# Column pieces of 704, 192 and 128 for the last row, and sums of their own in place of running sums

## The chip, the cores and the metric

The kernel runs on one core of one Trainium2 chip. The metric is the time of one execution in microseconds (us) on the device. Before the change it was 164.64 us (median of 3 runs, 164.58 to 164.67). A second measure is the **tail**, the time from the landing of row 14 of the last tile to the moment the store is issued. Both ends are in every trace, the landing as the last increment of that load's semaphore.

## The reference

```python
def reference(x):                      # x: (32, 512, 1024) float32
    relu_x = np.maximum(x, 0)
    return np.mean(relu_x, axis=-1).astype(np.float32)      # (32, 512)
```

16,384 rows of 1,024 numbers: each of the 128 partitions (the first dimension of every on-chip tile) takes 128 rows.

## The kernel before

Seven tiles of 16 rows stream in whole, and an eighth, the last one, in pieces. Rows alternate between ScalarE (`act_row`) and VectorE (`dve_row`); each is one instruction that applies the relu and adds up the row. Both engines follow it with a short instruction that reads the accumulator out. The last tile's pieces are of 8, 4, 2 and 1 rows, and its last row comes in column pieces, so that little work is left when the last byte has landed.

```python
def dve_row(nc, src, acc, init=None):
    nc.vector.tensor_scalar(out=src, in0=src, scalar1=0.0, scalar2=init,
                            op0=ALU.max, op1=ALU.add, accum_out=acc)
# ... (cut: tiles, loads of whole tiles)
    row_pieces = [8, 4, 2, 1]
    col_pieces = [512, 256, 256]
# ... (cut: the loads are issued here; rows 0 to 13 of the last tile)
    act_row(nc, prev[:, :512], part[:, 0:1])               # row 14, half each
    dve_row(nc, prev[:, 512:], part[:, 1:2])
    nc.gpsimd.tensor_scalar(out=res[:, J - 2:J - 1], in0=part[:, 0:1], scalar1=part[:, 1:2], scalar2=inv, op0=ALU.add, op1=ALU.mult)
    act_row(nc, last[:, :256], part[:, 2:3])               # row 15, piece 1
    dve_row(nc, last[:, 256:512], part[:, 3:4])
    nc.gpsimd.tensor_scalar(out=part[:, 4:5], in0=part[:, 2:3], scalar1=inv, scalar2=0.0, op0=ALU.mult, op1=ALU.add)
    act_row(nc, last[:, 512:640], part[:, 5:6])            # piece 2
    dve_row(nc, last[:, 640:768], part[:, 6:7], init=part[:, 3:4])
    nc.scalar.activation(out=part[:, 7:8], in_=part[:, 5:6], func=ACT.Identity, scale=inv, bias=part[:, 4:5])
    dve_row(nc, last[:, 768:], part[:, 8:9], init=part[:, 6:7])   # piece 3
    nc.vector.scalar_tensor_tensor(out=res[:, J - 1:J], in0=part[:, 8:9], scalar=inv, in1=part[:, 7:8], op0=ALU.mult, op1=ALU.add)
    nc.sync.dma_start(out=outr, in_=res)
```

The sums of VectorE form a chain: piece 2 starts from the sum of piece 1 (`init`), piece 3 from that of piece 2.

## Time and profile before

| what | value | where read |
|---|---|---|
| span of the profiled execution | 162.6 us | head of the page |
| DMA | 84% of the chain that ended last, 413 GB/s | chain, slices |
| VectorE, ScalarE busy | 46%, 43% | busy table |
| landing of row 14 | 157.81 us | semaphore records |
| landings of the three column pieces, after row 14's | +0.641, +0.994, +1.300 us | semaphore records |
| store issued, after row 14's landing (the tail) | +2.340 us | timeline |

From the page of the kernel before, the DMA engines' busy share in 40 slices of the span, in tenths, with what they moved, and below it the chain that ended last, first by engine and then by line:

```profile
DMA  7979989989988997997997998997998997998980
...
DMA packets 2162, 67.19 MB, mean 413 GB/s; under 512 B 240, under 2 KB 624, under 8 KB 880
```

```profile
DMA 84%; DVE 13%; SPq 1%; issue 0%; DVEq 0%
DMA xt<-in_x_dram 84%; DVE xt L20 13%; SPq L80 1%; SPq L72 0%; DVE res L112 0%; DVEq L20 0%; DVEq L112 0%
```

In the chain, a q behind an engine's name means its sequencer (SPq is that of SyncE), and L20 is the line inside `dve_row`. The DMA row stands at 0.7 or more in all but the last slice: the load stream sets the time. The change doesn't touch the stream, only its last 512 KB and what is computed on them. So everything at stake lies in the tail, 2.3 us of 162.6. Its timeline before (start in us, duration, engine, line, operation, out<-in; in brackets the idle time before, with its releaser):

```profile
157.83 0.69 DVE L20 TENSOR_SCALAR_CACHE_REDUCE xt<-xt 128x512 f32<-128x512 f32 x1
...
158.44 0.08 DVE L20 DVE_READ_ACCUMULATOR xt<-xt 128x1 f32 x1
...
158.47 0.42 DVE L20 TENSOR_SCALAR_CACHE_REDUCE xt<-xt 128x256 f32<-128x256 f32 x1
...
158.82 0.08 DVE L20 DVE_READ_ACCUMULATOR xt<-xt 128x1 f32 x1
...
158.93 0.35 DVE L20 TENSOR_SCALAR_CACHE_REDUCE xt<-xt,part 128x128 f32<-128x128 f32 x1
159.06 0.19 POOL L103 TENSOR_SCALAR part<-part 128x1 f32<-128x1 f32 x1
...
159.21 0.08 DVE L20 DVE_READ_ACCUMULATOR xt<-xt,part 128x1 f32 x1
159.32 0.48 DVE L20 TENSOR_SCALAR_CACHE_REDUCE xt<-xt,part 128x256 f32<-128x256 f32 x1
159.36 0.29 ACT L108 ACTIVATE part<-part 128x1 f32<-128x1 f32 x1
159.73 0.08 DVE L20 DVE_READ_ACCUMULATOR xt<-xt,part 128x1 f32 x1
159.92 0.16 DVE L112 SCALAR_TENSOR_TENSOR res<-part 128x1 f32<-128x1 f32 x1
160.15 0.35 SPq L115 DMA_DIRECT2D out_dram<-res  x1
```

Read it by VectorE (DVE). The second number of a reduction is longer than the time it holds the engine: the accumulator read starts before the reduction's record ends. What counts is from start to the start of the read: 613 ns for 512 columns, 345 for 256. A reduction that takes a running sum (`xt,part`) starts only after the read before it has ended, and takes 404 ns where the independent one of the same size took 345. Piece 3 landed at 159.11 us, but VectorE came to it at 159.32. Once it has begun on the last row, right on the first piece's landing (158.45), VectorE never again waits for data. GpSimd (L103) and ScalarE (L108) end by 159.66, with slack.

### The profile page before, as it was taken

How to read it: one execution, taken by the hardware profiler on the slowest of the kernel's cores; microseconds unless marked ns; L12 is line 12 of the kernel's file. 1: busy time of each engine (PE TensorE's matmuls, PEld its weight loads, DVE VectorE, ACT ScalarE, POOL GpSimd, SP SyncE). 2: the span in 40 equal slices, each digit the busy share in tenths (PEclk: the TensorE clock that was granted, in tenths of full speed). 3: DMA queues.
4: the chain of work that ended last, by engine and by line, in shares of the span. 5: the costliest groups of instructions: out<-in, count | busy, mean ns of one | idle time of the engine just before them, and what ended most of it. 6: DMA issues, size and time to landing. Idle time of an engine off the chain costs nothing.

```text
span 162.6 us, 358 instructions
## 1 busy us (share of the span) xinstructions
DVE 74.8 (46%) x135; ACT 69.6 (43%) x134; POOL 1.2 (1%) x8
## 2 busy tenths in 40 slices
DVE  0000039900696008940099201990049800698993
ACT  3000039700694008920099002980049600696882
POOL 0000000000000000000000000000000000000001
DMA  7979989989988997997997998997998997998980
GB/s 258 516 322 451 516 355 419 516 371 403 516 387 387 516 435 339 516 435 339 516 484 326 484 484 355 451 500 339 451 500 355 435 516 306 451 435 379 415 334 17
DMA packets 2162, 67.19 MB, mean 413 GB/s; under 512 B 240, under 2 KB 624, under 8 KB 880
## 3 DMA queue, kind: packets, MB, share of 16 engines
q1 hardware_dynamic: 2160, 67.18, 96.2%
q14 instruction: 2, 0.02, 0.0%
HBM read 67.11 MB, written 0.07 MB: 413 GB/s over the span
## 4 chain that ended last, share of the span: by engine, by line
DMA 84%; DVE 13%; SPq 1%; issue 0%; DVEq 0%
DMA xt<-in_x_dram 84%; DVE xt L20 13%; SPq L80 1%; SPq L72 0%; DVE res L112 0%; DVEq L20 0%; DVEq L112 0%
## 5 line engine op out<-in xcount | busy, mean ns | idle before, releaser
L20 DVE TENSOR_SCALAR_CACHE_REDUCE xt<-xt 128x1024 f32<-128x1024 f32 (+1 forms) x65 | 73.7, 1195 | 85.1 <-DMA xt<-in_x_dram 84.8
L15 ACT ACTIVATE xt<-xt 128x1024 f32<-128x1024 f32 (+1 forms) x66 | 67.0, 1016 | 89.2 <-DMA xt<-in_x_dram 89.2
L15 ACT ACTIVATION_READ_ACCUMULATOR xt<-xt 128x1 f32 x66 | 12.3, 187 | 0.0
L20 DVE DVE_READ_ACCUMULATOR xt<-xt 128x1 f32 x65 | 5.4, 83 | 0.0
L65 POOL TENSOR_SCALAR res<-sums 128x112 f32<-128x112 f32 (+1 forms) x2 | 0.5, 252 | 157.2 <-DVE xt L20 157.2
L15 ACT ACT_TABLE_LOAD x1 | 1.3, 1283 | 0.7 <-PEq L130 0.7
L20 DVE TENSOR_SCALAR_CACHE_REDUCE xt<-xt,part 128x128 f32<-128x128 f32 (+1 forms) x2 | 0.8, 412 | 0.1
L108 ACT ACTIVATE part<-part 128x1 f32<-128x1 f32 x1 | 0.3, 294 | 0.1
L98 POOL TENSOR_SCALAR res<-part 128x1 f32<-128x1 f32 x1 | 0.3, 264 | 0.6 <-ACT xt L15 0.6
L112 DVE SCALAR_TENSOR_TENSOR res<-part 128x1 f32<-128x1 f32 x1 | 0.2, 159 | 0.1
L103 POOL TENSOR_SCALAR part<-part 128x1 f32<-128x1 f32 x1 | 0.2, 191 | 0.1
L20 DVE DVE_READ_ACCUMULATOR xt<-xt,part 128x1 f32 x2 | 0.2, 83 | 0.0
L130 POOL MEMSET const-bfloat16-1.0<- 128x1 bf16 x1 | 0.1, 101 | 0.0
L130 POOL MEMSET const-uint8-127<- 128x1 uint8 x1 | 0.1, 101 | 0.0
L130 POOL MEMSET const-float32-0.0<- 128x1 f32 x1 | 0.1, 98 | 0.2 <-issue 0.2
L130 POOL MEMSET const-float32-1.0<- 128x1 f32 x1 | 0.1, 98 | 0.0
## 6 DMA issues: line engine op xcount, KB each, us to landing
xt<-in_x_dram SPq DMA_DIRECT2D x1, 4096.0 KB, 39.0
xt<-in_x_dram SPq DMA_DIRECT2D x1, 2048.0 KB, 43.5
xt<-in_x_dram SPq DMA_DIRECT2D x1, 1024.0 KB, 45.5
xt<-in_x_dram SPq DMA_DIRECT2D x1, 512.0 KB, 46.4
xt<-in_x_dram SPq DMA_DIRECT2D x1, 256.0 KB, 46.5
xt<-in_x_dram SPq DMA_DIRECT2D x2, 128.0 KB, 42.7
xt<-in_x_dram SPq DMA_DIRECT2D x7, 49.0
out_dram<-res SPq DMA_DIRECT2D x1, 64.0 KB, 1.5
```

Source lines behind the costliest of these rows:

```text
L15: nc.scalar.activation(out=src, in_=src, func=ACT.Relu, accum_out=acc)
L20: nc.vector.tensor_scalar(out=src, in0=src, scalar1=0.0, scalar2=init, op0=ALU.max, op1=ALU.add, accum_out=acc,)
L65: nc.gpsimd.tensor_scalar(out=res[:, lo:hi], in0=sums[:, lo:hi], scalar1=inv, scalar2=0.0, op0=ALU.mult, op1=ALU.add,)
L80: nc.sync.dma_start(out=xt[:, lo:lo + n, :], in_=xr[:, j0 + lo:j0 + lo + n, :])
L98: nc.gpsimd.tensor_scalar(out=res[:, J - 2:J - 1], in0=part[:, 0:1], scalar1=part[:, 1:2], scalar2=inv, op0=ALU.add, op1=ALU.mult,)
L103: nc.gpsimd.tensor_scalar(out=part[:, 4:5], in0=part[:, 2:3], scalar1=inv, scalar2=0.0, op0=ALU.mult, op1=ALU.add,)
L108: nc.scalar.activation(out=part[:, 7:8], in_=part[:, 5:6], func=ACT.Identity, scale=inv, bias=part[:, 4:5],)
L112: nc.vector.scalar_tensor_tensor(out=res[:, J - 1:J], in0=part[:, 8:9], scalar=inv, in1=part[:, 7:8], op0=ALU.mult, op1=ALU.add,)
L130: nc = _bacc.Bacc("TRN2", target_bir_lowering=False, num_devices=1)
```

## The change

Its intent: a smaller last piece (128 columns), no running sums on VectorE, no ScalarE work behind the first piece, and GpSimd adding up the parts beside VectorE's last reduction.

```diff
-    col_pieces = [512, 256, 256]
+    col_pieces = [704, 192, 128]
@@
-    act_row(nc, last[:, :256], part[:, 2:3])
-    dve_row(nc, last[:, 256:512], part[:, 3:4])
+    act_row(nc, last[:, :416], part[:, 2:3])
+    dve_row(nc, last[:, 416:704], part[:, 3:4])
+    dve_row(nc, last[:, 704:896], part[:, 4:5])
     nc.gpsimd.tensor_scalar(
-        out=part[:, 4:5], in0=part[:, 2:3], scalar1=inv, scalar2=0.0, op0=ALU.mult, op1=ALU.add,
+        out=part[:, 5:6], in0=part[:, 4:5], scalar1=part[:, 3:4], scalar2=part[:, 2:3], op0=ALU.add, op1=ALU.add,
     )
-    act_row(nc, last[:, 512:640], part[:, 5:6])
-    dve_row(nc, last[:, 640:768], part[:, 6:7], init=part[:, 3:4])
-    nc.scalar.activation(
-        out=part[:, 7:8], in_=part[:, 5:6], func=ACT.Identity, scale=inv, bias=part[:, 4:5],
-    )
-    dve_row(nc, last[:, 768:], part[:, 8:9], init=part[:, 6:7])
-    nc.vector.scalar_tensor_tensor(
-        out=res[:, J - 1:J], in0=part[:, 8:9], scalar=inv, in1=part[:, 7:8], op0=ALU.mult, op1=ALU.add,
+    dve_row(nc, last[:, 896:], part[:, 6:7])
+    nc.vector.tensor_scalar(
+        out=res[:, J - 1:J], in0=part[:, 6:7], scalar1=part[:, 5:6], scalar2=inv, op0=ALU.add, op1=ALU.mult,
     )
```

## The prediction

> What bounds it now. The page's chain that ended last is 84% load, 13% VectorE; the slice table shows the DMA engines at 0.8 to 1.0 and 413 GB/s to the end, while VectorE is busy 46% and ScalarE 43%. Only the tail can move, from row 14's landing (157.81 us by the trace's semaphore records) to the store's issue at 160.15, 2.3 us of a 162.6 us span.
>
> The tail before, from the timeline and the semaphore records. The column pieces landed at 158.45, 158.80 and 159.11. VectorE ran 512 columns of row 14 (157.83), 256 (158.47, right on its landing), 128 with a running sum (158.93), 256 with a running sum (159.32), the closing operation (159.92 to 160.08); the store issued at 160.15. After the last landing VectorE needed 0.98 us. ScalarE's and GpSimd's parts were done by 159.66, with slack.
>
> What the change does.
> 1. Landings. Rows of 2048, 1024 and 512 B took 84, 46 and 27 ns each in the trace; 2816 B and 768 B should take about 112 and 36 (estimate by interpolation), eight rows per engine. The same total; the landings become about 158.67, 158.93, 159.12. The first piece comes 0.22 us later, the last unchanged.
> 2. VectorE. A reduction with no running sum reaches its accumulator read after 80 ns plus n columns/0.96 ns (613 ns at 512, 345 at 256), and the next independent one starts there. A running-sum operand costs 59 ns more (404 against 345 at 256) and about 110 ns waiting for the earlier read; both go away. So (estimates) 288 columns 158.69 to 159.07, 192 to 159.34, 128 to 159.56, read done 159.64. Before, the last read was done at 159.81. The Trainium skill's "VectorE: DVE Perf Modes" (The TRN2 errata) states a fixed latency per SBUF instruction plus columns at 0.96 GHz; the trace agrees in slope, with 80 ns for its 58 cycles. VectorE gets 608 columns of the last row instead of 640, in three instructions either way.
> 3. ScalarE. 416 columns end with their read at 159.32, off the path.
> 4. GpSimd. The add waits for the 192-column sum, read at 159.42. Earlier GpSimd operations with two waits started 0.15 us after their last input, and took 0.19 us without and 0.26 with one per-partition operand; with two I estimate 0.33. So 159.57 to 159.91, and the closing operation starts about 159.97, not at 159.75 where VectorE alone would allow it. This is the new critical step, and takes back 0.2 us. The skill's "Perfetto Trace Analysis" (GPSIMD Engine Instruction) calls such spans unreliable, so this is my least sure term.
> 5. Closing operation: a per-partition operand, about 0.16 + 0.06 = 0.22 us, ending near 160.19, 0.1 us later than now. The store has one wait fewer ahead of it (0.03 us saved), issue near 160.22.
>
> Net: +0.07 us: VectorE's gain (0.17) is lost to GpSimd's late add. Predicted 164.7 us; 8 in 10 between 164.3 and 165.1 (mostly run and chip variation). Faster by over 2%: 0.01; within 2%: 0.98; slower by over 2%: 0.01.
>
> Shown right or wrong by: three VectorE reductions of the last row back to back with no gap; the closing operation released by GpSimd; VectorE idle about 0.2 us between its last accumulator read and the closing operation; first landing near 158.67, last near 159.12; store issue within 0.15 us of 160.2.
>
> What would make it wrong: GpSimd starting or finishing 0.2 us faster, which would make it about 0.1 us faster than before; landings of odd-sized rows (2816, 768 B) costing more than interpolated; the loads, 157 us, differing between runs by more than the whole tail.

## The result

The changed kernel took 164.69 us (median of 4 runs, 164.59 to 165.03); the kernel before, in the same rounds, 164.65 (4 runs). The ratio is 1.0007, with a 95% interval of 0.9989 to 1.0024: the same within what these runs resolve. (A ratio is the mean time of one kernel's fast runs over that of the other's of the same rounds, so it is not quite the ratio of the medians.) Five further rounds (e1) gave 1.0010 (0.9998 to 1.0022).

The load stream is unchanged: 413 GB/s over the span, before and after. The traces resolve more than the times. The tail grew from 2.340 to 2.476 us. From the page after, the chain by engine and line:

```profile
DMA 84%; DVE 12%; SPq 1%; issue 0%; POOLq 0%; DVEq 0%
DMA xt<-in_x_dram 84%; DVE xt L20 12%; SPq L80 1%; POOLq L137 0%; SPq L72 0%; DVE res L108 0%; DVEq L20 0%; POOLq L104 0%
```

GpSimd's sequencer (POOLq L104, the wait ahead of its add, and POOLq L137, a line of the launch code, which runs beside the add) has entered the chain, which it was not part of before; the end of the kernel now passes through it. The list of waits after names who waited for whom (us in total, times, longest):

```profile
POOL part L104 <- DVE xt L20: 0.7, 1, 0.7
...
DVE res L108 <- POOL part L104: 0.4, 1, 0.4
```

The tail after, to be held against the timeline before:

```profile
158.82 0.45 DVE L20 TENSOR_SCALAR_CACHE_REDUCE xt<-xt 128x288 f32<-128x288 f32 x1 [0.21 <-DMA xt<-in_x_dram]
159.20 0.08 DVE L20 DVE_READ_ACCUMULATOR xt<-xt 128x1 f32 x1
159.20 0.35 DVE L20 TENSOR_SCALAR_CACHE_REDUCE xt<-xt 128x192 f32<-128x192 f32 x1
...
159.47 0.08 DVE L20 DVE_READ_ACCUMULATOR xt<-xt 128x1 f32 x1
159.47 0.28 DVE L20 TENSOR_SCALAR_CACHE_REDUCE xt<-xt 128x128 f32<-128x128 f32 x1
159.68 0.08 DVE L20 DVE_READ_ACCUMULATOR xt<-xt 128x1 f32 x1
159.73 0.36 POOL L104 TENSOR_SCALAR part<-part 128x1 f32<-128x1 f32 x1 [0.68 <-DVE xt L20]
160.13 0.21 DVE L108 TENSOR_SCALAR res<-part 128x1 f32<-128x1 f32 x1 [0.37 <-POOL part L104]
160.37 0.35 SPq L111 DMA_DIRECT2D out_dram<-res  x1
```

VectorE now does 288, 192 and 128 columns with no gap: each reduction starts at the instant the accumulator read before it starts. But it first sits idle 0.21 us for the first piece, and after its last sum it sits idle 0.37 us before the closing operation, which waits for GpSimd's add (0.36 us long); that could start only when the 192-column sum had been read out.

Measured from each trace's own landing of row 14, in us:

| step | before | after, predicted | after, measured |
|---|---|---|---|
| first column piece landed | 0.641 | 0.86 | 0.900 |
| last column piece landed | 1.300 | 1.31 | 1.301 |
| VectorE's last accumulator read ended | 2.005 | 1.83 | 1.863 |
| GpSimd's add started, ended | | 1.76, 2.10 | 1.836, 2.201 |
| closing operation started, ended | 2.117, 2.276 | 2.16, 2.38 | 2.235, 2.448 |
| store issued (tail) | 2.340 | 2.41 | 2.476 |

The row of the predicted column is the prediction's time less 157.81, the landing that it started from.

### The profile page after: what moved, and what is told of

It is laid out like the page before. It is cut to its first block, busy times and chain, and to the rows that moved or that the text cites. A ratio compares the mean times of both kernels' runs of the same rounds, so it can differ in the third digit from the quotient of the medians.

```text
span 162.8 us, 353 instructions
## 1 busy us (share of the span) xinstructions
DVE 74.5 (46%) x135; ACT 69.2 (43%) x131; POOL 1.3 (1%) x8
## 4 chain that ended last, share of the span: by engine, by line
DMA 84%; DVE 12%; SPq 1%; issue 0%; POOLq 0%; DVEq 0%
DMA xt<-in_x_dram 84%; DVE xt L20 12%; SPq L80 1%; POOLq L137 0%; SPq L72 0%; DVE res L108 0%; DVEq L20 0%; POOLq L104 0%
## 5 line engine op out<-in xcount | busy, mean ns | idle before, releaser
L20 DVE TENSOR_SCALAR_CACHE_REDUCE xt<-xt 128x1024 f32<-128x1024 f32 (+2 forms) x67 | 74.2, 1169 | 85.5 <-DMA xt<-in_x_dram 85.1
L65 POOL TENSOR_SCALAR res<-sums 128x112 f32<-128x112 f32 (+1 forms) x2 | 0.5, 248 | 157.3 <-DVE xt L20 157.3
L104 POOL TENSOR_SCALAR part<-part 128x1 f32<-128x1 f32 x1 | 0.4, 365 | 0.7 <-DVE xt L20 0.7
```

The source lines that it names most:

```text
L65: nc.gpsimd.tensor_scalar(out=res[:, lo:hi], in0=sums[:, lo:hi], scalar1=inv, scalar2=0.0, op0=ALU.mult, op1=ALU.add,)
L104: nc.gpsimd.tensor_scalar(out=part[:, 5:6], in0=part[:, 4:5], scalar1=part[:, 3:4], scalar2=part[:, 2:3], op0=ALU.add, op1=ALU.add,)
```

## The experiments

The theory after the two traces: the change is two halves that cancel. The new pieces cost time, because the first one lands later and VectorE was behind the loads anyway; the new sums save time on VectorE and lose it to GpSimd. Rivals: that GpSimd's add is the only cost; that it costs nothing; that the tail is hidden behind something else, so that the equal times say nothing.

Runs e1 to e4 shared one chip, e5 to e8 a second, e9 and e10 a third; for the first two traces the record names no chip. Most kernels have one trace. The landings of the column pieces after row 14's agree within 0.04 us between traces of the same pieces, except in e10, so a difference of tails much smaller than that says nothing. The tails, from each trace:

| run | pieces | sums | tail us | median us | ratio to before (95% interval) |
|---|---|---|---|---|---|
| before | 512, 256, 256 | running | 2.340 | 164.65 | |
| e9, before again | 512, 256, 256 | running | 2.340 | 164.66 | 0.9998 (0.9985 to 1.0012) |
| after | 704, 192, 128 | own, GpSimd adds | 2.476 | 164.69 | 1.0007 (0.9989 to 1.0024) |
| e1, after again | 704, 192, 128 | own, GpSimd adds | 2.462 | 164.78 | 1.0010 (0.9998 to 1.0022) |
| e2 | 704, 192, 128 | running | 2.454 | 164.72 | 1.0013 (0.9997 to 1.0028) |
| e3 | 512, 256, 256 | own, GpSimd adds | 2.269 | 164.67 | 1.0000 (0.9984 to 1.0015) |
| e4 | 704, 192, 128 | own, one VectorE sum | 2.199 | 164.60 | 0.9994 (0.9982 to 1.0007) |
| e5 | 704, 192, 128 | own, GpSimd adds, copies 4 times | 3.557 | 165.82 | 1.0075 (1.0056 to 1.0093) |
| e6 (wrong on purpose) | 704, 192, 128 | own, GpSimd reads one sum | 2.212 | 164.37, one run | |
| e7 | 512, 384, 128 | own, one VectorE sum | 2.070 | 164.49 | 0.9988 (0.9974 to 1.0002) |
| e8 | 512, 256, 256 | own, one VectorE sum | 2.032 | 164.27 | 0.9980 (0.9963 to 0.9997) |
| e10 | 704, 192, 128 | own, VectorE adds | 2.488 | 165.11, one run | |

### e1: the changed kernel again

No edit.

> The changed kernel once more, on the chip that runs the next three. Yardstick for all runs, since the load stream alone moves by 0.1 us: the time from the landing of row 14 to the issue of the store ('tail'), 2.34 us in the trace of the kernel before and 2.48 us in that of the changed one. My theory (two opposite halves): tail 2.48 +-0.05, the time within 0.2% of before. Rival (the tail is hidden, and the times differ by the load stream alone): the same here.

The tail was 2.462 us, 0.014 from the first trace, with row 14 landing 0.2 us later. The tail is thus a measure that repeats; the time alone, with runs from 164.38 to 165.12 of the kernel before in these rounds, would not have shown a difference of 0.13 us.

### e2: the new pieces alone

```diff
# against the kernel before; the other lines that go, and GpSimd's, ScalarE's and the closing operation as before, are cut
-    col_pieces = [512, 256, 256]
+    col_pieces = [704, 192, 128]
# the running sums of before, at the new borders:
+    act_row(nc, last[:, :416], part[:, 2:3])
+    dve_row(nc, last[:, 416:704], part[:, 3:4])
+    act_row(nc, last[:, 704:800], part[:, 5:6])
+    dve_row(nc, last[:, 800:896], part[:, 6:7], init=part[:, 3:4])
+    dve_row(nc, last[:, 896:], part[:, 8:9], init=part[:, 6:7])
```

> The new column pieces 704, 192, 128 under the old running sums (192 split 96 and 96 between ScalarE and VectorE). Theory of two opposite halves: VectorE starts on the last row 0.26 us later and its chain of running sums is as long as before, so the tail is 2.6 us (2.5 to 2.7), 0.28 over before and 0.14 over the changed kernel. Rival (GpSimd's late add is the only thing that the change costs): no GpSimd add on the path here, the last landing is unchanged, so the tail is at most 2.4.

The tail was 2.454: longer than before by 0.114 us, where I expected 0.28. From this run's timeline, VectorE's reductions and the end:

```profile
158.93 0.45 DVE L20 TENSOR_SCALAR_CACHE_REDUCE xt<-xt 128x288 f32<-128x288 f32 x1 [0.19 <-DMA xt<-in_x_dram]
159.30 0.08 DVE L20 DVE_READ_ACCUMULATOR xt<-xt 128x1 f32 x1
...
159.42 0.31 DVE L20 TENSOR_SCALAR_CACHE_REDUCE xt<-xt,part 128x96 f32<-128x96 f32 x1
...
159.78 0.35 DVE L20 TENSOR_SCALAR_CACHE_REDUCE xt<-xt,part 128x128 f32<-128x128 f32 x1
...
160.47 0.35 SPq L115 DMA_DIRECT2D out_dram<-res  x1
```

The direction held, and the rival's bound (at most 2.4) failed. The size was off because the expectation took the chain of running sums to be "as long as before". It isn't: VectorE has 128 columns less to do, which at the 1.05 ns a column of the trace before (613 less 345 ns for 256 columns) is 0.13 us. VectorE starts on the last row 0.24 us later than before (0.906 against 0.665 after row 14's landing). The difference of the two is 0.11. The wait of a running sum is as before, 0.03 to 0.04 us after the end of the read that it needs (the read at 159.30 took 0.083, the next reduction starts at 159.42), that is about 0.12 after the read's start.

### e3: the new sums alone

```diff
-    col_pieces = [704, 192, 128]
+    col_pieces = [512, 256, 256]
-    act_row(nc, last[:, :416], part[:, 2:3])
-    dve_row(nc, last[:, 416:704], part[:, 3:4])
-    dve_row(nc, last[:, 704:896], part[:, 4:5])
+    act_row(nc, last[:, :256], part[:, 2:3])
+    dve_row(nc, last[:, 256:512], part[:, 3:4])
+    dve_row(nc, last[:, 512:768], part[:, 4:5])
-    dve_row(nc, last[:, 896:], part[:, 6:7])
+    dve_row(nc, last[:, 768:], part[:, 6:7])
```

> The old column pieces 512, 256, 256 under the new structure (ScalarE 256, VectorE 256, 256 and 256 with sums of their own, GpSimd's add, one closing operation). Theory of two opposite halves: tail 2.27 us (2.15 to 2.35), 0.07 under before and 0.2 under the changed kernel, with the closing operation still released by GpSimd and VectorE idle some 0.23 us before it. Rival (GpSimd's late add is the only cost): it is in this kernel too, so the tail is about 2.45 to 2.5 as in the changed kernel.

The tail was 2.269 against the 2.27 expected: 0.071 better than before, although VectorE has 768 columns of the last row here and had 640 before. The rival, which expected 2.45 to 2.5, failed. From its timeline, VectorE's reductions, GpSimd's add and the end:

```profile
158.57 0.42 DVE L20 TENSOR_SCALAR_CACHE_REDUCE xt<-xt 128x256 f32<-128x256 f32 x1
...
158.93 0.42 DVE L20 TENSOR_SCALAR_CACHE_REDUCE xt<-xt 128x256 f32<-128x256 f32 x1
159.28 0.08 DVE L20 DVE_READ_ACCUMULATOR xt<-xt 128x1 f32 x1
159.28 0.41 DVE L20 TENSOR_SCALAR_CACHE_REDUCE xt<-xt 128x256 f32<-128x256 f32 x1
159.54 0.36 POOL L104 TENSOR_SCALAR part<-part 128x1 f32<-128x1 f32 x1 [0.48 <-DVE xt L20]
...
159.94 0.21 DVE L108 TENSOR_SCALAR res<-part 128x1 f32<-128x1 f32 x1 [0.24 <-POOL part L104]
160.18 0.35 SPq L111 DMA_DIRECT2D out_dram<-res  x1
```

VectorE sits idle 0.24 us before the closing operation here too, but the sum that GpSimd waits for is ready earlier, because VectorE could begin at 158.57, right behind row 14. With this the two halves stand alone: the new sums bring 0.071 us on the old pieces and nothing on the new ones (2.454 against 2.462 and 2.476); the new pieces cost 0.114 us under the old sums and 0.193 to 0.207 under the new ones. So the halves do not simply cancel. On the new pieces the new sums end VectorE's last read 0.25 us earlier (1.863 against 2.111 after row 14's landing, in e2), and GpSimd takes all of it back: the closing operation starts at 2.235 against 2.232. The traces also say why the third piece of 128 columns was worth nothing under the new sums; no run varied it alone. The end hangs on the second piece's sum, through GpSimd; up to there VectorE has 288 + 192 = 480 columns of the new pieces and 256 + 256 = 512 of the old, 0.03 us apart, while the start differs by 0.24 to 0.26.

### e4: no GpSimd add

```diff
-    nc.gpsimd.tensor_scalar(
-        out=part[:, 5:6], in0=part[:, 4:5], scalar1=part[:, 3:4], scalar2=part[:, 2:3], op0=ALU.add, op1=ALU.add,
-    )
-    dve_row(nc, last[:, 896:], part[:, 6:7])
+    dve_row(nc, last[:, 896:], part[:, 5:6])
     nc.vector.tensor_scalar(
-        out=res[:, J - 1:J], in0=part[:, 6:7], scalar1=part[:, 5:6], scalar2=inv, op0=ALU.add, op1=ALU.mult,
+        out=part[:, 2:6], in0=part[:, 2:6], scalar1=inv, scalar2=None, op0=ALU.mult, op1=ALU.add,
+        accum_out=res[:, J - 1:J],
     )
```

The four sums lie side by side, and one reduction of four columns scales and adds them.

> The changed kernel without GpSimd's add: the four sums lie side by side, and one VectorE reduction scales and adds them after the 128-column piece. Theory (GpSimd's add is the last wait, worth 0.3 us): tail 2.17 us (2.1 to 2.25), closing reduction released by VectorE's own last sum, 0.3 us less than the changed kernel in the time as well (ratio to before about 0.999). Rival (VectorE's gap before the closing operation is the wait for its own last accumulator read and the store's issue, so GpSimd costs nothing): tail 2.4 to 2.5.

The tail was 2.199 (expected 2.17), 0.26 to 0.28 under the changed kernel's. The rival, 2.4 to 2.5, failed. The end of its timeline:

```profile
159.60 0.28 DVE L20 TENSOR_SCALAR_CACHE_REDUCE xt<-xt 128x128 f32<-128x128 f32 x1
159.81 0.08 DVE L20 DVE_READ_ACCUMULATOR xt<-xt 128x1 f32 x1
160.01 0.16 DVE L105 TENSOR_SCALAR_CACHE_REDUCE part<-part 128x4 f32<-128x4 f32 x1
160.10 0.08 DVE L105 DVE_READ_ACCUMULATOR part<-part 128x1 f32 x1
160.24 0.35 SPq L109 DMA_DIRECT2D out_dram<-res  x1
```

Between the end of the last accumulator read (159.81 + 0.08) and the closing reduction lie 0.12 us, which VectorE's wait for its own sum costs and which the kernel before has too (0.11). So of the 0.37 us idle in the changed kernel some 0.25 were GpSimd's. The closing operation is another one here, but from its start to the store's issue it takes 0.23 us against 0.24, so the gain is not from that. The kernel is correct. Its time, ratio 0.9994, is not resolved from 1.

### e5: four more GpSimd operations

```diff
+    # x4: part[:, 7:8] <- part[:, 5:6], 8 <- 7, 9 <- 8, 5 <- 9
+    nc.gpsimd.tensor_scalar(
+        out=part[:, 7:8], in0=part[:, 5:6], scalar1=1.0, scalar2=0.0, op0=ALU.mult, op1=ALU.add,
+    )
```

> The changed kernel with four copies by GpSimd, each of the one before, between its add and the closing operation (the result is the same). Theory (GpSimd's last operation releases the closing operation, and the tail counts one to one in the time): four times 0.19 busy and 0.08 handoff, so the tail is about 3.55 us (3.3 to 4.1) and the time 1.0 to 1.6 us above the changed kernel's 164.7 (ratio to before 1.006 to 1.010). Rival (the tail is hidden behind something else at the end of the run, so the equal times say nothing about the tail): the tail grows, the time does not.

The tail was 3.557 us, 1.08 to 1.10 over the changed kernel's, and the time 165.82 us, about 1.1 us over it (by the medians, from other rounds); the ratio to before is clear of 1. The rival is out: the tail goes one to one into the time. From the timeline, GpSimd's five operations and the closing one:

```profile
159.89 0.36 POOL L104 TENSOR_SCALAR part<-part 128x1 f32<-128x1 f32 x1 [0.66 <-DVE xt L20]
160.34 0.19 POOL L107 TENSOR_SCALAR part<-part 128x1 f32<-128x1 f32 x1
160.62 0.19 POOL L110 TENSOR_SCALAR part<-part 128x1 f32<-128x1 f32 x1
160.89 0.19 POOL L113 TENSOR_SCALAR part<-part 128x1 f32<-128x1 f32 x1
161.16 0.19 POOL L116 TENSOR_SCALAR part<-part 128x1 f32<-128x1 f32 x1
161.39 0.21 DVE L120 TENSOR_SCALAR res<-part 128x1 f32<-128x1 f32 x1 [1.47 <-POOL part L116]
```

The starts are 0.27 us apart where each takes 0.19 by its own record: a dependent operation on GpSimd costs 0.08 us besides its length. The Trainium skill, "Perfetto Trace Analysis" (GPSIMD Engine Instruction), asks to treat a GpSimd span in a profile as unreliable and to go by the spacing of starts. The two fit: the spacing is the span of 0.19 and a handoff of 0.08, and the next run shows 0.08 again between the end of a VectorE read and GpSimd's start. As the handoff is what is left of the spacing, this is no independent test of the span.

### e6: GpSimd's operation without per-partition operands

Its output is wrong, which doesn't matter for the time. The operation reads one sum and two constants.

```diff
-        out=part[:, 5:6], in0=part[:, 4:5], scalar1=part[:, 3:4], scalar2=part[:, 2:3], op0=ALU.add, op1=ALU.add,
+        out=part[:, 5:6], in0=part[:, 4:5], scalar1=1.0, scalar2=0.0, op0=ALU.mult, op1=ALU.add,
```

> Wrong result on purpose: GpSimd's add reads one sum and two constants in place of three sums, so it has no per-partition operand and one wait. Theory (its length is set by the two per-partition operands, 0.36 against 0.19 us without, and its two waits add 0.06 us before its start): it starts about 0.08 us after the 192-column sum's read ends, takes 0.19 us, and the tail is 2.22 us (2.15 to 2.3), near that of the kernel with no GpSimd add (2.20). Rival (the handoffs between engines are the cost, whatever the operation reads): tail 2.4 or more.

The tail was 2.212 us, as expected (2.22), and the rival's 2.4 failed. GpSimd's operation and the end:

```profile
159.68 0.19 POOL L104 TENSOR_SCALAR part<-part 128x1 f32<-128x1 f32 x1 [0.58 <-DVE xt L20]
...
159.92 0.21 DVE L108 TENSOR_SCALAR res<-part 128x1 f32<-128x1 f32 x1
160.16 0.35 SPq L111 DMA_DIRECT2D out_dram<-res  x1
```

It took 0.19 us in place of 0.365 and started 0.08 us after the read that it waits for, in place of 0.18; the closing operation is again held by VectorE's own last sum, if narrowly (GpSimd's end and a handoff of 0.034 us would have let it start 0.01 us sooner). The same handoff with one input instead of three is harmless, so its cost in the changed kernel is the two operands in its length (0.17 us) and the later start (0.10 us). This run takes away the second wait and the operands at once. GpSimd's earlier operation at L65, with two waits and no operand, started 0.16 us after its last input in the traces before and after, so most of the 0.10 goes with the second wait; the rest was not separated.

### e7 and e8: versions meant to beat both

Early first piece as before, sums of their own on both engines, no GpSimd, and the closing reduction of e4.

```diff
# e7 (in both diffs the lines that go are cut)
+    col_pieces = [512, 384, 128]
+    act_row(nc, last[:, :256], part[:, 2:3])
+    dve_row(nc, last[:, 256:512], part[:, 3:4])
+    act_row(nc, last[:, 512:704], part[:, 4:5])
+    dve_row(nc, last[:, 704:896], part[:, 5:6])
+    dve_row(nc, last[:, 896:], part[:, 6:7])
# e8
+    col_pieces = [512, 256, 256]
+    act_row(nc, last[:, :256], part[:, 2:3])
+    dve_row(nc, last[:, 256:512], part[:, 3:4])
+    act_row(nc, last[:, 512:640], part[:, 4:5])
+    dve_row(nc, last[:, 640:768], part[:, 5:6])
+    act_row(nc, last[:, 768:832], part[:, 6:7])
+    dve_row(nc, last[:, 832:], part[:, 7:8])
# both: one VectorE reduction over part[:, 2:7] or part[:, 2:8], as in e4
```

> A version meant to beat both: pieces 512, 384, 128; ScalarE 256 and 192, VectorE 256, 192 and 128, five sums of their own side by side, and one VectorE reduction that scales and adds them. Theory (early first piece, no running sum, no GpSimd): tail 2.08 us (2.0 to 2.15), 0.26 under before and 0.38 under the changed kernel; time 0.1 to 0.4 us under before, which five rounds may not resolve. Rival (the first piece's landing does not matter, only GpSimd does): tail 2.2, as with the pieces 704, 192, 128.

> The same idea on the old pieces 512, 256, 256: ScalarE 256, 128 and 64, VectorE 256, 128 and 192, six sums, one closing reduction. Theory: VectorE starts its last 192 columns on their landing; tail 2.04 us (1.95 to 2.15), bounded by ScalarE's last read and VectorE's last read about equally. Rival as before: tail 2.2.

The tails were 2.070 and 2.032 us (expected 2.08 and 2.04); the rival's 2.2 failed. Both versions also move work to ScalarE: VectorE has 576 columns of the last row, where e4 has 608, 0.03 us by its rate. So not all of the 0.13 and 0.17 us to e4 is the first piece's landing; e4's sums on the old pieces, with nothing else changed, were not run. The end of e8's timeline:

```profile
159.32 0.35 DVE L20 TENSOR_SCALAR_CACHE_REDUCE xt<-xt 128x192 f32<-128x192 f32 x1
...
159.52 0.19 ACT L15 ACTIVATION_READ_ACCUMULATOR xt<-xt 128x1 f32 x1
159.60 0.08 DVE L20 DVE_READ_ACCUMULATOR xt<-xt 128x1 f32 x1
159.81 0.16 DVE L107 TENSOR_SCALAR_CACHE_REDUCE part<-part 128x6 f32<-128x6 f32 x1
...
160.04 0.35 SPq L111 DMA_DIRECT2D out_dram<-res  x1
```

In e8, VectorE begins its last 192 columns at 159.32, 0.02 us after they landed (1.293 after row 14's landing at 158.01): alone among these kernels its last reduction waits for the data, and not the other way round. Its times, 164.27 us in the median against 164.68 of before in the same rounds, give a ratio of 0.9980 (0.9963 to 0.9997), just clear of 1 (of the nine such intervals here, one may be so by chance); the tails give 0.308 us, 0.19% of 164.65, which agrees. e7's 0.9988 agrees with its tail too (0.27 us, 0.16%), but its interval holds 1.

### e9: the kernel before again

No edit.

> The kernel before, against itself: the noise floor of five rounds and a second trace of it. Theory: tail 2.34 us (2.30 to 2.38), ratio 1.000 with an interval about 0.0015 to either side, so that the changed kernel's +0.13 us of tail (0.08%) is below what the times resolve. Rival (the changed kernel's extra tail is scatter between traces): this tail is off 2.34 by 0.1 or more.

The tail was 2.340 us again, in a trace whose row 14 landed 0.44 us later than in the first. The ratio of the kernel to itself was 0.9998 (0.9985 to 1.0012). So the changed kernel's 0.12 to 0.14 us of tail are real, and five rounds of times, with intervals of some 0.2 us to either side, could not show them.

### e10: the add on VectorE (inconclusive)

```diff
-    nc.gpsimd.tensor_scalar(
+    dve_row(nc, last[:, 896:], part[:, 6:7])
+    nc.vector.tensor_scalar(
         out=part[:, 5:6], in0=part[:, 4:5], scalar1=part[:, 3:4], scalar2=part[:, 2:3], op0=ALU.add, op1=ALU.add,
     )
-    dve_row(nc, last[:, 896:], part[:, 6:7])
```

> The changed kernel with the same three-sum add on VectorE, behind the 128-column reduction. Theory (the cost is GpSimd's start after two waits and its 0.36 us; VectorE does the same add in 0.28 us and needs no handoff, but it now stands in VectorE's own line): tail 2.40 us (2.30 to 2.45), 0.06 under the changed kernel. Rival (an added step before the closing operation costs the same on any engine): tail 2.46 or more.

The tail was 2.488 us. The theory's 2.30 to 2.45 failed and the rival's 2.46 or more held. But the kernel on the chip was not the one that I meant: the build had moved the add ahead of the 128-column reduction, which then waited behind it (the add started at 160.11 and the reduction at 160.30). Also, in this single run the column pieces landed 0.06 us closer to row 14 than in the other traces of these pieces. What it would cost to place the add behind the last reduction stays open; e4's closing reduction makes the question moot.

## Why the prediction was right

It said 164.7 us, the same within 2%, and 164.69 was measured. That alone proves little, as a change confined to a tail of 2.3 us can't do much to 164.6: almost any mechanism would have met this range. Of the checks that it named, two held plainly (three reductions with no gap; the closing operation released by GpSimd). The idle time of "about 0.2 us" was missed (0.37). "Store issue within 0.15 us of 160.2" was missed by the clock of the trace (160.37) and held from row 14's landing (2.476 against 2.39), which came 0.09 us later than in the trace before; the landings of the first and last piece (158.80 and 159.20, not 158.67 and 159.12) are late mostly for the same reason. Its counterfactual held: with GpSimd's add done more than 0.2 us sooner (e6) the tail was 0.13 us shorter than before, where it had said about 0.1. The mechanism can be checked step by step:

1. **Landings.** Predicted 0.22 us later for the first piece and unchanged for the last; measured 0.26 and 0.00 (0.24 in e1). Rows of 2816 and 768 bytes took 112 and 36 ns in the trace, as interpolated.
2. **VectorE.** Three reductions back to back, as predicted. The gain at the last accumulator read was 0.142 us against the 0.17 predicted, smaller by the late landing. The prediction drew on the Trainium skill, "VectorE: DVE Perf Modes" (The TRN2 errata), for a fixed cost per instruction plus columns at 0.96 GHz. This trace agrees in the slope (273 and 206 ns for 192 and 128 columns, 1.05 ns a column); the fixed part up to the accumulator read was about 80 ns, or 73 in reductions that began straight with the read before them, not the page's 58 cycles (60 ns).
3. **ScalarE** was off the path, as predicted: its read ended at 159.46 us, before the 192-column sum that GpSimd waited for as well (159.56).
4. **GpSimd releases the closing operation**, as predicted; e4, e5 and e6 show it by taking the add away, lengthening it and thinning it. Two sizes were short: the start after the two waits (0.18 us, not 0.15) and the length (0.365 us, not 0.33). The prediction's check "VectorE idle about 0.2 us" was a slip: its own times give 0.33 (159.64 to 159.97); 0.37 was measured, of which some 0.25 were GpSimd's (e4).
5. **Closing operation.** 0.213 us against 0.22 predicted; the store was issued 0.03 us after it, as predicted.

The net was predicted at +0.07 us of tail and was +0.136 (+0.122 in e1). The missing 0.06 are 0.04 of the landing and 0.03 each of GpSimd's start and length, less about 0.03 of the handoff from GpSimd to VectorE, which took 0.034 us and not the 0.06 supposed. What the prediction didn't say is that the third piece's small size had become worthless, since the end hung on the second piece's sum; the traces of the changed kernel and e3 show that. And it named the loss as GpSimd's alone ("VectorE's gain (0.17) is lost to GpSimd's late add"). In fact the new pieces, with their later first landing, cost 0.11 to 0.21 us by themselves (e2 against before, after against e3), so even with GpSimd gone (e4, 2.199) the new pieces stay 0.17 us behind the old ones with the same closing reduction (e8, 2.032; that run also shares the columns out differently between the engines, so it is not the pieces alone).

## What to carry to other kernels

Make the last piece of a load smaller where the consumer waits for that piece; where the consumer is behind the loads, as VectorE was here (0.2 us after the last landing it had not begun on the data), what counts is how early the first piece lands and how much work each engine has. A helper engine takes work off the critical engine only if its result is ready before it is wanted: count its start after its last input, its operands and the handoff back. When a change is small against the scatter of the times, find a start and an end in the trace between which nothing else varies, and compare that; here it repeated to 0.015 us in two kernels traced twice, where the times scattered by half a microsecond. Check the steps in between too: in e10 the landings inside the tail had moved by 0.06.

## What the Trainium skill lacked or had wrong

- "GPSIMD Engine Reference" and "Perfetto Trace Analysis" give no cost for a small operation with per-partition operands. On 128x1 numbers it took 0.19 us with none, 0.26 with one, 0.365 with two; it started 0.08 us after its last input where it had one wait (e6), 0.16 us after it with two waits and no operand (L65, on 14 columns), and 0.18 us after it with two waits and two operands (changed kernel).
- "Perfetto Trace Analysis" (GPSIMD Engine Instruction) calls GpSimd spans unreliable. For these operations they repeated (0.19 us in e5 and e6, 0.36 to 0.37 in every trace of the three-sum add) and fitted the spacing of starts, 0.27 us (e5); that doesn't test the span by itself, so the page isn't shown to be wrong.
- "VectorE: DVE Perf Modes" (the perf-mode tier table) gives no rate for `tensor_scalar` with an accumulator output. Here it ran at one fp32 column per cycle of 0.96 GHz (345 ns at 256 columns, 613 at 512), with a read of 83 ns behind it.
- The same page (The DRAIN you can't avoid) says that a semaphore between VectorE operations costs nothing extra. That was measured on copies. Here a reduction that waits for the accumulator read of the one before starts 0.12 us after that read's start, and one that doesn't wait starts with it; the running-sum operand itself adds 59 ns (404 against 345).
- No page that I read has the cheap way to close many sums: one VectorE reduction over sums that lie side by side, 0.17 us from its start to the end of its accumulator read for 4 to 6 sums (e4, e7, e8).
